# Eight of 31 convolution taps as diagonal products on TensorE, and a written-out order for VectorE beside the query, key and value products

## The chip, the cores and the metric

The program runs on one core of a Trainium2 chip. The metric is the device time of one execution in microseconds (us). A core has TensorE (PE, matrix products, 128x128 array that can be addressed in tiles of 32x32), VectorE (DVE), ScalarE (ACT), GpSimd (POOL) and SyncE (SP), which here issues the DMAs. Each engine runs its instructions in the order in which they stand in its queue, and semaphores order the engines against each other. SBUF is the working memory. PSUM, where TensorE writes its results, has eight banks of 128 partitions x 512 fp32 columns; POOL can't read it.

## The reference, cut to what matters

The model is a stack of blocks in fp32; the change touches the first mixer only. It takes 512 latent and 256 context rows of 1024 features (768 rows in all), projects them, and forms a convolution branch and query, key and value:

```python
def conformer_conv(p_glu, conv_w, conv_b, ln_g, ln_b):
    a, gate = jnp.split(p_glu, 2, axis=-1)
    u = depthwise_conv(a * jax.nn.sigmoid(gate), conv_w, conv_b)   # 31 taps, 512 channels
    return jax.nn.silu(layer_norm(u, ln_g, ln_b))
...
    conv_lat = conformer_conv(p_lat[..., :EV_Q0], conv_w, conv_b, ln_g, ln_b)
    q_lat = apply_axial_rope(qk_heads(p_lat[..., EV_Q0:EV_K0]), rope)
    k_lat = apply_axial_rope(qk_heads(p_lat[..., EV_K0:EV_V0]), rope)
    v_lat = v_heads(p_lat[..., EV_V0:])
```

The attention over all 768 keys follows, and the output projection takes the convolution and the attention side by side. Context rows go through the same convolution, without rotation of q and k.

## The kernel before, in words

Features lie on the 128 partitions, rows on the columns. An fp32 product is made of three fp32r products of high and low halves (`mm3`, lines 90 to 92). `wsplit` (line 60) loads a weight tile of 512 KB into `wraw` (3 buffers), ACT makes its high half `whi` (line 73), and DVE, or POOL where told, its low half `wlo` (line 74), two buffers of each. Before it loads, it advances a background generator by two steps: `mods` (line 146) makes modulation vectors, each from eight steps that load 512 KB of `ada_w` into `wraw` and run two fp32 products on 32-column strips of the array (line 153), and a ninth with a copy, four small products (line 160) and a DVE add (line 161).

`even_mixer` (line 355) first makes the gated input `us` of the convolution in four chunks of 128 channels (lines 414 to 424); beside it the generator `fg` makes the filters of a later block (`hyena_spectra`; its DVE lines here are 705, 719, 725 and 726, and its PSUM pool `evf` has 2 banks). Then comes the stage that the change touches. In it three streams are interleaved:

- `taps()` (line 437): per chunk, tap 0 has been made with the bias at line 424; taps 1 to 28 are 28 DVE instructions at line 449 over 128 x 798 columns (768 rows and the padding), each adding `us`, shifted by the tap, times a column of weights to `conv[i]`. Taps 29 and 30 are made by ACT (lines 443 and 446), POOL adds these two (line 447) and adds their sum to the chunk (line 452). After the fourth chunk `conv_norm` makes the layer norm over the channels and the SiLU, for 512 and then for 256 columns (lines 457 to 484). It is a generator that is advanced once or twice per product.
- eight q and k products: `wsplit`, 24 matmuls of 512 columns, rotation by three DVE instructions (494 to 496) and a POOL add (497), then 24 matmuls of 256 columns, copied by ACT (499). For the last four POOL makes the low half of the weight.
- twelve V products of 24 matmuls with 256 columns, two groups of six, each group with two weight tiles; ACT copies the results (511).

PSUM banks are handed out from below in the order in which pools are opened: `ps` has 4 banks, `mps` 2, `evf` 2 while the filters are made, and `cps`, for conv_norm, these 2 after it. Attention then opens pools over the same eight banks, with its score tiles `S` on banks 4 to 7. SBUF of pool `evp`, which the three streams use, lies where the filter generator's pool lay.

Nothing in the program fixes the order of the queues: a planner orders the instructions of all engines by program order and by its own model of durations, so that a later instruction may run ahead of an earlier one that waits.

Of the kernel before, what the change touches and what calls it, by code (L numbers as in the profile page):

```python
# [10 lines left out]
F32 = mybir.dt.float32  # L11
# [3 lines left out]
ALU = mybir.AluOpType  # L15
AX = mybir.AxisListType
PSUM = bass.MemoryType.PSUM

D = 1024
T = 512  # L20
C = 256
# [5 lines left out]
def f32(ap):  # L27
    return ap.bitcast(F32)

# [325 lines left out]
def even_mixer(k, xc):  # L355
    nc, a = k.nc, k.a
    regs = [(0, T), (T, C)]
# [8 lines left out]
    with ExitStack() as es:  # L366
        hp = es.enter_context(ExitStack())
        cp = es.enter_context(k.pool("evc"))
        tp_ = hp.enter_context(k.pool("evt", side="right"))
        ps = hp.enter_context(k.pool("evps", 4, space=PSUM))  # L370
        mps = hp.enter_context(k.pool("evmps", 2, space=PSUM))
# [4 lines left out]
        with k.pool("hyf") as hy, k.pool("evf", 2, space=PSUM) as fps:  # L376
# [5 lines left out]
            with k.pool("evn") as np_:  # L382
                rbs = [k.norm_stats([t], [rg], ps, np_)[0] for t, rg in zip((xl, xc), regs)]
                with k.pool("ada", side="right") as mp:
                    for i, _ in enumerate(chain(k.mods(0, 1, mps, mp, 12), k.mods(0, 0, mps, mp, 12))):
                        if i == 3:
                            next(fg)
                h1 = hp.enter_context(k.pool("evh", side="right"))
                hh = h1.tile([128, 8, TC], F32R, name="hh")
# [42 lines left out]
        def b3(dt=F32):  # L432
            return k.tmp([128, TC], "b3", dt, 8, vp)

        qk = [b3() for i in range(8)]
        with k.pool("evp") as pp, k.behind([k.mods(0, kind, mps) for kind in (2, 3, 4)], 2):
            def taps():

                for i in range(4):
# [8 lines left out]
                    for j in range(1, 29):  # L448
                        nc.vector.scalar_tensor_tensor(out=o, in0=u[:, j:j + W], scalar=cw[:, i, j:j + 1], in1=o, op0=ALU.mult, op1=ALU.add)
                        if j == 14:  # L450
                            yield
                    nc.gpsimd.tensor_tensor(out=o, in0=o, in1=o2, op=ALU.add)
# [33 lines left out]
            cps = hp.enter_context(k.pool("evcps", 2, space=PSUM))  # L486
            tg = taps()
            rope = k.cload("rope2d", [128, 2, T], pool=pp)
            for i in range(8):
                w = k.wsplit(a["ev_w_fm"][8 + i], eng=nc.gpsimd if i >= 4 else None)  # L490
                acc = k.gemm(w, h, 8, 0, T, ps)
                t1 = k.tmp([128, T], "rt1", bufs=1, pool=pp)
                t2 = k.tmp([128, T], "rt2", bufs=2, pool=pp)
                nc.vector.stream_shuffle(t2, acc, [(j + 16) % 32 for j in range(32)])
                nc.vector.tensor_tensor(out=t1, in0=acc, in1=rope[:, 0], op=ALU.mult)
                nc.vector.tensor_tensor(out=t2, in0=t2, in1=rope[:, 1], op=ALU.mult)
                nc.gpsimd.tensor_tensor(out=qk[i][:, 0:T], in0=t1, in1=t2, op=ALU.add)
                acc = k.gemm(w, h, 8, T, C, ps)
                nc.scalar.copy(qk[i][:, T:], acc)
                next(tg)  # L500
            for g in range(2):
                vb = [k.wsplit(a["ev_w_v"][g, kq * 4:kq * 4 + 4].rearrange("k p f -> p k f")) for kq in range(2)]
                for t in range(6):
                    acc = k.tmp([128, 512], "acc", pool=ps, bufs=None)[:, :256]
                    for kt in range(8):
                        s = slice(kt % 4 * 256, kt % 4 * 256 + 256)
                        w = vb[kt // 4]
                        k.mm3(acc, (hh[:, kt, t * 128:(t + 1) * 128], hl[:, kt, t * 128:(t + 1) * 128]),
                              (w[0][:, s], w[1][:, s]), kt == 0, kt == 7)
                    s = slice(g * 256, g * 256 + 256)  # L510
                    nc.scalar.copy(vv[:, t, s], acc)
                    if t % 3 == 2:
                        next(tg, None)
# [1737 lines left out]
```

## Time and profile before

| | us |
|---|---|
| median of 3 runs | 3662.72 (3659.55 to 3664.95) |
| the profiled execution | 3663.87, span 3662.1 |
| PE busy | 3421.9 (93% of the span) |
| DVE busy | 2431.2 (66%) |
| ACT busy | 1460.6 (40%) |
| POOL busy | 665.8 (18%) |

All times in the rows are counted from the start of the span. An engine's busy time is the union of its instructions, so that matmuls which overlap are counted once; `PEld` are TensorE's weight loads. `PEclk` is the granted clock of TensorE as a share of its full 2.4 GHz. An fp32 matmul leaves two records, an fp32r matmul one. The stage that the change touches lies between about 160 and 360 us.

### The profile page before, as it was taken

What the parts mean: (1) busy time and instruction counts of PE and PEld (TensorE: products, weight loads), DVE (VectorE), ACT (ScalarE), POOL (GpSimd) and SP (SyncE); (2) the same over time, 40 slices, a digit from 0 to 9 for tenths busy, and PEclk for the clock granted to TensorE, in tenths of its full rate; (3) what the DMA queues carried; (4) which work ended last, traced back from release to release, by engine and by line L of the source; (5) the groups of instructions that cost most, each with busy time, mean ns of one, the idle gap of its engine ahead of it and who ended that gap; (6) DMA issues with size and microseconds to landing.
All of it is one profiled execution on the core that took longest, in us unless ns stands there. A gap on an engine that the chain in (4) does not pass through costs nothing.

```text
span 3662.1 us, 54926 instructions
## 1 busy us (share of the span) xinstructions
PE 3421.9 (93%) x21924; PEld 2820.3 (77%) x21924; DVE 2431.2 (66%) x3995; ACT 1460.6 (40%) x2525; POOL 665.8 (18%) x587
## 2 busy tenths in 40 slices
PE   6987989999998899889999999999999999999999
PEld 3765878888887667667888877767998877777998
DVE  7997876544458765654334676657877676757886
ACT  4223543222226434323223444543444544644443
POOL 0042101102102332311111032021111032012110
PEclk9997999999999999889999999999999999999999
DMA  6334114333333222332223313232333313232333
GB/s 212 110 120 114 38 52 129 113 123 119 118 102 122 79 76 78 119 103 80 93 92 98 107 58 104 92 121 81 103 105 104 109 50 119 73 132 83 103 98 98
DMA packets 156842, 369.31 MB, mean 101 GB/s; under 512 B 19207, under 2 KB 44167, under 8 KB 156200
## 3 DMA queue, kind: packets, MB, share of 16 engines
q1 hardware_dynamic: 156584, 365.79, 31.5%
q8 instruction: 172, 2.82, 0.3%
q14 instruction: 86, 0.70, 0.1%
HBM read 334.27 MB, written 28.31 MB: 99 GB/s over the span
## 4 chain that ended last, share of the span: by engine, by line
PE 42%; DVE 12%; issue 6%; ACT 4%; POOL 2%; DMA 1%; SPq 0%; DVEq 0%; POOLq 0%; ACTq 0%
PE acc L90 12%; PE acc L92 12%; PE acc L91 12%; DVE wlo L74 1%; DMA wraw<-in_w_up_dram 1%; DVE hb L1614 1%; PE rec L1339 1%; PE rec L1340 1%; ACT whi L73 1%; DVE wslo L85 1%; PE acc L1416 1%; PE acc L1415 1%; DVE oz L830 1%; PE acc L1417 1%; ACT mp L1849 0%
## 5 line engine op out<-in xcount | busy, mean ns | idle before, releaser
L73 ACT CAST whi<-wraw 128x1024 fp32r<-128x1024 f32 (+2 forms) x442 | 408.0, 923 | 862.0 <-PE acc L91 664.4
L74 DVE TENSOR_TENSOR wlo<-wraw,whi 128x1024 fp32r<-128x1024 f32 (+2 forms) x438 | 487.1, 1112 | 185.4 <-ACT whi L73 180.7
L90 PE MATMUL acc<-hh,whi 128*128 128x512 f32 (+1 forms) x1024 | 367.4, 359 | 11.8 <-ACT whi L73 6.4
L92 PE MATMUL acc<-hh,wlo 128*128 128x512 f32 (+1 forms) x1024 | 364.9, 357 | 12.2 <-POOL wlo L74 8.8
L91 PE MATMUL acc<-hl,whi 128*128 128x512 f32 (+1 forms) x1024 | 365.8, 358 | 2.7 <-DVE hl L256 2.3
L91 PE MATMUL acc<-hidl,whi 128*128 128x512 f32 (+1 forms) x768 | 274.2, 357 | 1.6 <-DVE hidl L85 1.6
L92 PE MATMUL acc<-hidh,wlo 128*128 128x512 f32 (+1 forms) x768 | 274.2, 357 | 0.6 <-DVE wlo L74 0.6
L90 PE MATMUL acc<-hidh,whi 128*128 128x512 f32 (+1 forms) x768 | 274.4, 357 | 0.0
L341 POOL TENSOR_TENSOR sqr<-relu 128x512 f32<-128x512 f32 (+1 forms) x96 | 127.8, 1332 | 689.3 <-ACT relu L339 685.8
L90 PEld LDWEIGHTS acc<-hh,whi 128*128 128x128 f32 x1024 | 196.2, 192 | 50.9 <-ACT whi L73 10.2
L92 PEld LDWEIGHTS acc<-hh,wlo 128*128 128x128 f32 x1024 | 195.5, 191 | 47.0 <-POOL wlo L74 10.1
L91 PEld LDWEIGHTS acc<-hl,whi 128*128 128x128 f32 x1024 | 196.9, 192 | 35.4 <-DVE hl L256 5.9
L92 PE MATMUL acc<-shh,wlo 128*128 128x512 f32 (+1 forms) x480 | 194.7, 406 | 7.2 <-DVE wlo L74 7.2
L90 PE MATMUL acc<-shh,whi 128*128 128x512 f32 (+1 forms) x480 | 196.1, 409 | 3.5 <-ACT whi L73 3.5
L91 PE MATMUL acc<-shl,whi 128*128 128x512 f32 (+1 forms) x480 | 194.8, 406 | 1.1 <-issue 1.1
L85 POOL TENSOR_TENSOR flo<-fth,fhi 128x512 fp32r<-128x512 f32 x44 | 82.3, 1870 | 531.4 <-ACT fhi L84 506.5
L90 PE MATMUL acc<-fsh,wshi 128*128 128x256 f32 x576 | 163.7, 284 | 4.4 <-ACT wshi L84 4.4
L91 PEld LDWEIGHTS acc<-hidl,whi 128*128 128x128 f32 x768 | 145.1, 189 | 25.2 <-DVE hidl L85 2.0
L92 PE MATMUL acc<-fsh,wslo 128*128 128x256 f32 x576 | 162.5, 285 | 1.5 <-DVE wslo L85 1.5
L91 PE MATMUL acc<-fsl,wshi 128*128 128x256 f32 x576 | 163.4, 284 | 0.0
L92 PEld LDWEIGHTS acc<-hidh,wlo 128*128 128x128 f32 x768 | 144.3, 188 | 23.9 <-DVE wlo L74 1.0
L191 DVE SCALAR_TENSOR_TENSOR mdacc<-wraw,cs,mdacc 128x1024 f32<-128x1024 f32 x70 | 94.4, 1372 | 102.6 <-DMA wraw<-in_ada_w_dram 102.6
(684 smaller groups left out, 9142.8 us busy)
## 6 DMA issues: line engine op xcount, KB each, us to landing
wraw<-in_mlp_w_dram SPq DMA_DIRECT2D x128, 512.0 KB, 3.5
wraw<-in_ada_w_dram SPq DMA_DIRECT2D x96, 512.0 KB, 4.0
wraw<-in_w_in_dram SPq DMA_DIRECT2D x58, 512.0 KB, 3.5
wraw<-in_od_w_fm_dram SPq DMA_DIRECT2D x36, 512.0 KB, 3.6
wraw<-in_w_gate_dram SPq DMA_DIRECT2D x72, 256.0 KB, 2.9
wraw<-in_w_up_dram SPq DMA_DIRECT2D x72, 256.0 KB, 3.1
wraw<-in_w_down_dram SPq DMA_DIRECT2D x48, 256.0 KB, 2.7
wraw<-in_w_down_dram SPq DMA_DIRECT2D x32, 320.0 KB, 2.9
```

Of the source, the lines that this page charges most:

```text
L73: nc.scalar.copy(hi, raw)
L74: (eng or nc.vector).tensor_tensor(out=lo, in0=raw, in1=f32(hi), op=ALU.subtract)
L85: (eng or nc.vector).tensor_tensor(out=lo, in0=src, in1=f32(hi), op=ALU.subtract)
L90: nc.tensor.matmul(out, s[0], m[0], start=first, stop=False)
L91: nc.tensor.matmul(out, s[0], m[1], start=False, stop=False)
L92: nc.tensor.matmul(out, s[1], m[0], start=False, stop=last)
L191: nc.vector.scalar_tensor_tensor(out=acc, in0=w, scalar=c, in1=acc, op0=ALU.mult, op1=ALU.add)
L341: nc.gpsimd.tensor_tensor(out=s, in0=r, in1=r, op=ALU.mult)
L830: nc.vector.scalar_tensor_tensor(out=o, in0=p[:, j:j + n], scalar=w[:, j:j + 1], in1=o, op0=ALU.mult, op1=ALU.add)
L1339: nc.tensor.matmul(op_[pf[d], hd], qd[:, c, pf[d]], S[:, c], start=True, stop=False)
L1340: nc.tensor.matmul(op_[pf[d], hd], at[pf[d], c], vn[pf[d], hd], start=False, stop=True)
L1415: nc.tensor.matmul(o, hh[:, kt, ts], w[0][:, ws], start=first, stop=False)
```

## The change

Of each chunk's 31 taps, 21 to 28 become products: `dia` holds for each of 32x32 blocks the diagonal of the tap's weights, and `strips` runs, per chunk and region, 4 blocks of channels x 4 tap groups on the 16 tiles of the array, twice, into four banks; ACT copies them out, and `joined` adds the four tap groups with the matrix `sum4` and adds the result to `conv[i]` on DVE. DVE keeps taps 1 to 20. The chunk's sum with taps 29 and 30 goes from POOL to DVE, as do the low halves of the last four q and k weights.

`ps` has three banks now, the modulations' pool `mps` is closed after the first two vectors and opened anew with one bank, and `cps`, with four, is opened ahead of the taps. The taps advance one instruction per step, and inside `manual_schedule` DVE executes the instructions in the order in which the program states them; other DVE instructions may fall between them, and the other engines are left to the planner. The next weight is loaded and split ahead of the taps of a product.

```diff
+P0, PT = 21, 8
...
-        ps = hp.enter_context(k.pool("evps", 4, space=PSUM))
-        mps = hp.enter_context(k.pool("evmps", 2, space=PSUM))
+        ps = hp.enter_context(k.pool("evps", 3, space=PSUM))
...
-                with k.pool("ada", side="right") as mp:
+                with k.pool("ada", side="right") as mp, k.pool("evmps", 2, space=PSUM) as mps:
...
+        mps = hp.enter_context(k.pool("evmps1", 1, space=PSUM))
+        cps = hp.enter_context(k.pool("evcps", 4, space=PSUM))
         with k.pool("evp") as pp, k.behind([k.mods(0, kind, mps) for kind in (2, 3, 4)], 2):
+            dia = pp.tile([128, 4, PT, 32], F32, name="cdia")
+            for i in range(4):
+                nc.gpsimd.tensor_tensor(out=dia[:, i], in0=k.sum4.unsqueeze(1).to_broadcast([128, PT, 32]),
+                                        in1=cw[:, i, P0:P0 + PT].unsqueeze(2).to_broadcast([128, PT, 32]), op=ALU.mult)
+            def strips(i, r):
+                c0, n = regs[r]
+                bank = [k.tmp([128, 512], "acc", pool=cps, bufs=None) for _ in range(4)]
+                for t in range(0, PT, 4):
+                    for s in range(4):
+                        for q in range(4):
+                            p = slice(32 * q, 32 * q + 32)
+                            u0 = c0 + 30 * r + P0 + t + s
+                            nc.tensor.matmul(bank[q][32 * s:32 * s + 32, :n], dia[p, i, t + s], us[p, i, u0:u0 + n], start=t == 0, stop=t + 4 >= PT)
+                e = k.tmp([128, 4, T], "cve", bufs=1, pool=pp)
+                for q in range(4):
+                    nc.scalar.copy(e[:, q, :n], bank[q][:, :n])
+                return i, r, e
+            def joined(i, r, e):
+                c0, n = regs[r]
+                acc = k.tmp([128, 512], "acc", pool=ps, bufs=None)[:, :n]
+                for q in range(4):
+                    nc.tensor.matmul(acc[32 * q:32 * q + 32], k.sum4, e[:, q, :n], start=True, stop=True)
+                o = conv[i][:, c0 + 30 * r:c0 + 30 * r + n]
+                nc.vector.tensor_tensor(out=o, in0=acc, in1=o, op=ALU.add)
...
-                    for j in range(1, 29):
+                    last = strips(i, 0)
+                    for j in range(1, P0):
                         nc.vector.scalar_tensor_tensor(out=o, in0=u[:, j:j + W], scalar=cw[:, i, j:j + 1], in1=o, op0=ALU.mult, op1=ALU.add)
-                        if j == 14:
-                            yield
-                    nc.gpsimd.tensor_tensor(out=o, in0=o, in1=o2, op=ALU.add)
+                        if j == P0 // 2:
+                            joined(*last)
+                            last = strips(i, 1)
+                        yield
+                    nc.vector.tensor_tensor(out=o, in0=o, in1=o2, op=ALU.add)
+                    joined(*last)
                     yield
...
-            for i in range(8):
-                w = k.wsplit(a["ev_w_fm"][8 + i], eng=nc.gpsimd if i >= 4 else None)
-                acc = k.gemm(w, h, 8, 0, T, ps)
...
-                next(tg)
...
+            with k.tc.manual_schedule(engines={mybir.EngineType.DVE}):
+                some(12)
+                w = k.wsplit(a["ev_w_fm"][8])
+                for i in range(8):
+                    accs = [k.gemm(w, h, 8, c0, n, ps) for c0, n in regs]
+                    if i < 7:
+                        w = k.wsplit(a["ev_w_fm"][9 + i])
+                    else:
+                        vb = [k.wsplit(a["ev_w_v"][0, kq * 4:kq * 4 + 4].rearrange("k p f -> p k f")) for kq in range(2)]
+                    some(5)
+                    acc = accs[0]
...
+                for g in range(2):
+                    for t in range(6):
...
+                        some(3 if g else 2)
+                    if g == 0:
+                        vb = [k.wsplit(a["ev_w_v"][1, kq * 4:kq * 4 + 4].rearrange("k p f -> p k f")) for kq in range(2)]
             for _ in tg:
                 pass
```

`some(n)` advances `taps()` by n steps. The rotation, the copies and the twelve V products are as before.

## Rows read from the trace of the kernel before

**Rows 1.** The page's first line.
```profile
span 3662.1 us, 54926 instructions
```
**Rows 2.** Stretches from 80 to 372 us, busy time of each engine.
```profile
core 0: us, PE busy (x) PEld busy (x) DVE busy (x) ACT busy (x) POOL busy (x), PEclk, DMA share, GB/s
80.00:160.00 80.00, 72.82 (x367) 58.22 (x366) 75.97 (x100) 23.80 (x37) 2.59 (x2) 0.96 0.27 86
160.00:191.00 31.00, 28.18 (x127) 18.05 (x126) 31.00 (x39) 5.45 (x7) 3.40 (x2) 1.00 0.52 170
191.00:296.00 105.00, 80.06 (x404) 57.44 (x404) 102.43 (x101) 19.20 (x26) 44.69 (x19) 0.85 0.36 116
296.00:352.00 56.00, 49.46 (x356) 44.30 (x356) 40.06 (x58) 22.46 (x41) 18.51 (x13) 0.88 0.50 140
```
**Rows 3.** The same for line 449 alone, the taps.
```profile
80.00:160.00 80.00, 29.90 (x29) 0.96 0.27 86
160.00:191.00 31.00, 9.81 (x9) 1.00 0.52 170
191.00:312.00 121.00, 96.30 (x74) 0.84 0.35 113
```
**Rows 4.** Timeline of TensorE: start, duration, engine, line, operation, idle before.
```profile
211.18 1.06 PE L153 MATMUL acc<-wraw,cs 128*32 128x512 f32 x8
...
212.17 0.50 PE L90 MATMUL acc<-hh,whi 128*128 128x512 f32 x1
...
217.87 0.28 PE L90 MATMUL acc<-hh,whi 128*128 128x256 f32 x1
...
220.70 0.95 PE L160 MATMUL acc<-c_ada_sel,wraw 128*128 128x4 f32 x8
...
251.09 0.79 PE L92 MATMUL acc<-hh,wlo 128*128 128x512 f32 x1 [8.28 <-POOL wlo L74]
...
354.74 0.77 PE L571 MATMUL S<-KS,QS 128*128 128x512 f32 x1 [1.10 <-issue]
```
**Rows 5.** Groups of POOL's instructions, 120 to 300 us: busy, mean ns | idle before.
```profile
L497 POOL TENSOR_TENSOR b<-rt,rt 128x512 f32<-128x512 f32 x8 | 15.8, 1980 | 28.5 <-DVE rt L496 28.5
...
L447 POOL TENSOR_TENSOR cw<-cw,cw 128x798 f32<-128x798 f32 x4 | 10.1, 2523 | 24.8 <-ACT cw L446 24.8
L452 POOL TENSOR_TENSOR conv<-conv,cw 128x798 f32<-128x798 f32 x3 | 7.7, 2565 | 19.3 <-DVE conv L449 19.2
```
**Rows 6.** Timeline of DVE.
```profile
117.46 8.73 DVE L449 SCALAR_TENSOR_TENSOR conv<-xl,c_ev_conv_w,conv 128x798 f32<-128x798 f32 x9
...
188.36 1.28 DVE L719 SCALAR_TENSOR_TENSOR hys<-acc,hyinv 128x512 f32<-128x512 f32 x2
...
295.23 1.21 DVE L74 TENSOR_TENSOR wlo<-wraw,whi 128x1024 fp32r<-128x1024 f32 x1
...
342.90 0.16 DVE L467 TENSOR_SCALAR ms<-acc 128x2 f32<-128x2 f32 x1 [0.67 <-PE acc L465]
...
352.98 1.66 DVE L479 SCALAR_TENSOR_TENSOR conv<-acc,c_ev_ln,conv 128x256 f32<-128x256 f32 x4
...
357.56 0.75 DVE L483 SCALAR_TENSOR_TENSOR conv<-cv,conv 128x256 f32<-128x256 f32 x2
```
**Rows 7.** Groups of DVE's instructions, 191 to 312 us.
```profile
L494 DVE STREAM_SHUFFLE rt<-acc 128x512 f32<-128x512 f32 x8 | 5.8, 737 | 0.0
L495 DVE TENSOR_TENSOR rt<-acc,c_rope2d 128x512 f32<-128x512 f32 x8 | 5.4, 678 | 0.5 <-POOL b L497 0.5
```
**Rows 8.** Timeline of TensorE in a later block.
```profile
1218.15 0.75 PE L1239 MATMUL prep<-R,LM 32*32 32x32 f32 x64
```
**Rows 9.** Groups of instructions by shape, 165 to 360 us.
```profile
L479 DVE SCALAR_TENSOR_TENSOR conv<-acc,c_ev_ln,conv 128x512 f32<-128x512 f32 x4 | 2.7, 744 | 1.1 <-PE acc L121 1.1
...
L157 ACT COPY wraw<-acc 128x512 f32<-128x512 f32 x3 | 1.8, 585 | 9.5 <-PE acc L153 9.5
...
L479 DVE SCALAR_TENSOR_TENSOR conv<-acc,c_ev_ln,conv 128x256 f32<-128x256 f32 x4 | 1.7, 477 | 0.0
```

More of the change, by code (lines that the diff above doesn't have):

```diff
@@ L484, in conv_norm @@
                 yield
-            cps = hp.enter_context(k.pool("evcps", 2, space=PSUM))
             tg = taps()
             rope = k.cload("rope2d", [128, 2, T], pool=pp)
-            for i in range(8):
-                w = k.wsplit(a["ev_w_fm"][8 + i], eng=nc.gpsimd if i >= 4 else None)
-                acc = k.gemm(w, h, 8, 0, T, ps)
[L492 to L499, printed above, removed]
-                next(tg)
@@ L501, in even_mixer, with some @@
[L501 to L513, printed above, removed]
+            def some(n):
+                for _ in range(n):
+                    next(tg, None)
@@ new lines, in even_mixer @@
+            with k.tc.manual_schedule(engines={mybir.EngineType.DVE}):
[9 more added lines that the diff above has]
+                    acc = accs[0]
+                    t1 = k.tmp([128, T], "rt1", bufs=1, pool=pp)
+                    t2 = k.tmp([128, T], "rt2", bufs=2, pool=pp)
+                    nc.vector.stream_shuffle(t2, acc, [(j + 16) % 32 for j in range(32)])
+                    nc.vector.tensor_tensor(out=t1, in0=acc, in1=rope[:, 0], op=ALU.mult)
+                    nc.vector.tensor_tensor(out=t2, in0=t2, in1=rope[:, 1], op=ALU.mult)
+                    nc.gpsimd.tensor_tensor(out=qk[i][:, 0:T], in0=t1, in1=t2, op=ALU.add)
+                    nc.scalar.copy(qk[i][:, T:], accs[1])
+                for g in range(2):
+                    for t in range(6):
+                        acc = k.tmp([128, 512], "acc", pool=ps, bufs=None)[:, :256]
+                        for kt in range(8):
+                            s = slice(kt % 4 * 256, kt % 4 * 256 + 256)
+                            w = vb[kt // 4]
+                            k.mm3(acc, (hh[:, kt, t * 128:(t + 1) * 128], hl[:, kt, t * 128:(t + 1) * 128]),
+                                  (w[0][:, s], w[1][:, s]), kt == 0, kt == 7)
+                        s = slice(g * 256, g * 256 + 256)
+                        nc.scalar.copy(vv[:, t, s], acc)
+                        some(3 if g else 2)
+                    if g == 0:
+                        vb = [k.wsplit(a["ev_w_v"][1, kq * 4:kq * 4 + 4].rearrange("k p f -> p k f")) for kq in range(2)]
```

## The prediction, made before the changed kernel ran

> **What bounds the kernel now.** I read the span first, then the busy time of each engine by stretch, then the vector engine (DVE) inside the stage that the change touches, then TensorE's long waits there. The profiled execution lasted 3663.87 us with a span of 3662.1 us [rows 1], 1.77 us around it; the median of the runs is 3662.72, so this execution lies 1.15 above it, and I take that off at the end. Over the kernel TensorE is busy nearly everywhere; this stage is one of the exceptions, and the reader is to see it in [rows 2]: from 191 to 296 us DVE works 102.43 of 105 us and TensorE only 80.06. DVE is the bound there, with the taps: 74 of the 112 tap instructions run in 191 to 312 and take 96.30 us [rows 3]. The other 38 had already run, 29 of them in 80 to 160 and 9 in 160 to 191, between instructions of the gate products and of the filter generator. TensorE's longest single wait, 8.28 us, is for a weight's low half that GpSimd (POOL) makes [rows 4]; POOL had stood 19.2 us behind taps, at the chunk sum of L452 [rows 5]. Once the taps are over, the V products and the convolution's norm run side by side (296 to 352), and attention begins when the norm lets go of its banks: the last reading of a broadcast bank by L479 ends at 352.98 + 1.66 = 354.64, and the second score tile starts at 354.74 [rows 4, 6]. So what counts is the time at which conv_norm ends.
>
> **Step 1, taps.** 32 of 112 tap instructions go. Nine in a row take 8.73 us [rows 6], so .97 each and 31 us in all. Added on DVE: four chunk sums that POOL did (estimate .9 each, just under a tap, which has the same width) and eight joining adds (.68 for 512 columns, as L495 takes [rows 7], and about .42 for 256, an estimate: 4.4 us), 8.0 us; and four weight halves at 1.21 that POOL made, 4.8 us. POOL loses these eight instructions, the products of `dia` come to it (four, early, beside nothing).
>
> **Step 2, strips.** A strip of 512 columns is 32 matmuls in two rounds of 16 array positions. The nearest row is L153: four fp32 matmuls of 512 columns on four column groups, eight records, take 1.06 us together [rows 4]. That positions on different rows of the array overlap too is shown by L1239, whose 64 records of 32x32 lie on four positions, no two on the same rows, and take .75 us [rows 8]. If all 16 overlap, a strip costs 2.1 us (1.1 for 256 columns); if only the four columns do, 8.5 and 4.2. I take the lower, since each of the two directions overlaps in its row; the two at once no row shows. `joined` is the pattern of L153 itself: 1.06 and .6. Together 4.9 us a chunk, 19.5 us on TensorE; the bad end is 57 us.
> The Trainium skill (TensorE: Matmul & The Clock Gate, Part 3: Packing small matmuls) states a 10.6-fold gain for 16 positions at 512 columns; by it a strip would be 32 x 1.06 / 10.6 = 3.2 us, an estimate, and the stage some 4 us longer. The sum does not use it.
>
> **Step 3, the given order.** Instructions keep their order on DVE. The first twelve taps stand before the low half of the first weight (w8), and behind tap 10 stands the joining add of strip (0,0). This strip needs four PSUM banks. With `ps` on banks 0 to 2 the filters' pool is 3 and 4, `evmps1` is 3 and `evcps` 4 to 7, so one strip bank, and the evicted copy's place in SBUF too, come free only with the filter generator. Its last two evictions end at 188.36 + 1.28 = 189.64 [rows 6]. So ten taps run early instead of 38 by 191, and behind the waiting add stand two taps, w8, and with it all eight products; TensorE and SP's weight loads wait for that.
> The generator ends earlier in exchange: DVE was busy all 31.00 us of 160 to 191 [rows 2], 9.81 of them in taps [rows 3], which now stand still. I give it 6 of these (between 0 and 9.8, since its matmuls, casts and POOL adds also follow one another): 183.6. Then strip 2.1, four copies by ACT at .585 [rows 9] 2.3, joined 1.06, add .68, semaphores about .5: 190.3. Two taps 2.0, w8 1.2: 193.5. There 68 taps are left, where 74 were left in the kernel before at 191, and no product has begun. Of the 32 taps saved, six remain as a gain at this point. In 80 to 160, 19 fewer taps can free at most the 7.2 us for which TensorE is idle there [rows 2], and a bank less in `ps` can take some back: I count 0 and keep -5 to +3 for the range.
>
> **Step 4, the eight products.** TensorE needs for one 217.87 - 212.17 = 5.70 and 220.70 - 217.87 = 2.83 [rows 4], two modulation steps .53 each, and 5 of a chunk's 21 steps of strips, 1.2: 10.8. DVE needs w 1.2, five taps 4.85, rotation .74 + 2 x .68 = 2.1 [rows 7], adds .5: 8.6, and more while POOL works beside it: the 74 taps took 96.30 us instead of 72, 24 us more under 44.69 us of POOL [rows 2, 3], about half a us each; POOL keeps 15.8 + 10.1 us [rows 5], so about 1.4 per product. 10.0 against 10.8: TensorE sets the pace and DVE, which can't pull later taps ahead, idles. Twice the add of the modulations (L161) stands ahead of a weight half and waits for a matmul behind a whole product: 3 us. 193.5 + 8 x 10.8 + 3 = 283.
>
> **Step 5, V.** The second V half needs the buffer of the last weight, free at 283, and five taps, rotation 7 and twelve steps stand behind it: cast and half 2.3, taps 17 x .97 = 16.5, rotation 2.1, adds 1.8, POOL 1: 306.7. Only then come the halves of the second V group, 2.4, then the last 20 taps, 19.4, adds 2.0, waits 1.5: 332. V ends on TensorE ahead of that, near 327, where in the kernel before it went on up to 352 [rows 2].
>
> **Step 6, the tail.** conv_norm now lies alone behind the taps, in order, and its four last steps each wait for two ACT instructions. The 256-column half took, from L467 at 342.90 to the end of L483 at 358.31, 15.4 us [rows 6], some 4 of it other work; its three sums add 1.2. The 512 half scales by L479's forms, 744 / 477 = 1.56 [rows 9]. I take 16 + 26 = 42 us (between 35 and 47): end at 374, the last bank 3.7 us earlier (358.31 - 354.64) at 370. Against 354.64 this is 16 us later. Little hides it: all four score banks are banks of `evcps`, and the output products need conv. After it the rest of the kernel is unchanged and bound by TensorE, so the shift stays. 3662.72 + 16 = 3679.
>
> **Rivals.** (a) DVE doesn't idle: TensorE and the weight loads keep ahead of it. For it speaks that POOL's waits, 8.28 us in one place, are gone. Then DVE's own work decides: from 193.5, 68 taps 66, eleven halves 13.3, rotations 16.7, adds 7.3, POOL 10, so 307, plus 42, less 3.7: 345, 9 us earlier than 354.64; with a generator 4 us earlier and a tail of 37 us 18 earlier. 3645 to 3654, middle 3650: faster. It decides from the point where the products' period falls below 10.0 us or the fixed halves arrive without the waits of step 5. Against it stands that each rotation waits for a product by its place in the order.
> (b) The tail is covered: conv_norm's four rotating banks free the first score tile some 10 us before the last one, so that TensorE takes scores while the norm ends, and half of DVE's idling goes: no change, 3662. Against it: the first output product needs conv.
> (c) The strips don't overlap on the rows: 57 - 19.5 = 38 us more on TensorE, about 25 on the path: 3704.
> That an edit does nothing at all I can exclude for the taps; the order on the other engines stays the planner's and can move it by some us either way.
>
> **Numbers.** The forecast 3679 (3669 to 3695) has .50, (a) .25, (b) .15, (c) .10. What a measurement can tell from no change is 0.2%, 7.3 us. Slower .60, same .15, faster .25. The range, 3640 to 3706, takes in (a) with its best tail and (c).
>
> **What would show it.** Right: the first joining add starts within 10 us after the filters' last eviction; at that point only ten taps have run; the first product starts after 190; a gap on TensorE of over 30 us, filled with norm matmuls alone, between the last V product and the first score; conv_norm over 35 us long. Strips near 2 us each show step 2. Wrong: a first product before 180, taps that end before 315, or scores that begin before 350; then (a) holds. A strip over 6 us is (c).

## The result, and the profile after

The changed kernel takes 3716.99 us (median of 4 runs, 3708.53 to 3722.84) against 3663.27 us of the kernel before on the same chip: ratio 1.0146, 95% interval 1.0123 to 1.0169, some 54 us slower. The forecast was 3679 in a range up to 3706: the direction is right, the size is three times too small. The profiled execution took 3713.8 us, 49.9 more than that of before. All of it arises ahead of attention: the first score matmul starts at 402.05 us instead of 352.69, 49.4 later, and from there to the end of the span both kernels need the same time (3712.0 - 402.05 = 3309.95, 3662.1 - 352.69 = 3309.41). Of the 49.4 us, 23.3 have gathered when the eighth product ends (294.0 against 270.7), and 26.1 between there and the first score.

The stretches of the changed kernel, busy time of each engine (as [rows 2]):
```profile
core 0: us, PE busy (x) PEld busy (x) DVE busy (x) ACT busy (x) POOL busy (x), PEclk, DMA share, GB/s
80.00:160.00 80.00, 73.09 (x356) 58.74 (x355) 56.57 (x79) 22.33 (x34) 2.58 (x2) 0.94 0.26 86
160.00:191.00 31.00, 22.16 (x107) 16.08 (x106) 23.94 (x30) 5.89 (x8) 6.75 (x6) 0.89 0.25 85
191.00:296.00 105.00, 97.33 (x806) 67.47 (x806) 67.47 (x80) 27.16 (x46) 16.97 (x11) 0.97 0.37 121
296.00:352.00 56.00, 53.61 (x525) 38.76 (x525) 41.26 (x44) 12.57 (x27) 2.03 (x1) 1.00 0.33 104
352.00:372.00 20.00, 7.75 (x49) 5.77 (x47) 17.59 (x22) 8.44 (x12) 6.06 (x4) 0.61 0.58 178
372.00:402.00 30.00, 7.99 (x32) 7.20 (x32) 19.56 (x36) 10.59 (x19) 9.69 (x9) 0.50 0.21 48
```
DVE and TensorE have changed places. From 191 to 296 DVE, which was full, is busy 67.47 of 105 us and TensorE 97.33. From 352 to 402, where TensorE had scores to do, it is busy 15.74 of 50 us at a granted clock of .61 and .50 (half is 1.2 of 2.4 GHz, the lower level): what is left is a join and the last modulation matmuls, until 356.2, and then the norm's small matmuls alone. The taps alone, line 487 (as [rows 3]):
```profile
80.00:160.00 80.00, 10.43 (x10) 0.94 0.26 86
160.00:191.00 31.00, 0.00 (x0) 0.89 0.25 85
```
Ten taps ran early where 38 had. DVE's timeline (as [rows 6]) then shows the path: the filters' last eviction, a wait for the first joining add (L471), the two taps and the low halves behind it, four waits behind the last product (5.12, 7.41, 4.94 and 1.12 us), the last add, and the norm's last reading of a bank:
```profile
188.73 1.37 DVE L770 SCALAR_TENSOR_TENSOR hys<-acc,hyinv 128x512 f32<-128x512 f32 x2
...
208.05 0.69 DVE L471 TENSOR_TENSOR conv<-acc,conv 128x512 f32<-128x512 f32 x1 [16.59 <-PE acc L469]
208.78 2.14 DVE L487 SCALAR_TENSOR_TENSOR conv<-xl,c_ev_conv_w,conv 128x798 f32<-128x798 f32 x2
210.83 2.35 DVE L78 TENSOR_TENSOR wlo<-wraw,whi 128x1024 fp32r<-128x1024 f32 x2
...
297.12 0.17 DVE L165 TENSOR_TENSOR mods<-acc,c_ada_b 128x16 f32<-128x16 f32 x1 [5.12 <-PE acc L164]
...
305.84 1.22 DVE L78 TENSOR_TENSOR wlo<-wraw,whi 128x1024 fp32r<-128x1024 f32 x1 [7.41 <-ACT whi L77]
...
335.82 1.23 DVE L78 TENSOR_TENSOR wlo<-wraw,whi 128x1024 fp32r<-128x1024 f32 x1 [4.94 <-ACT whi L77]
...
356.21 0.17 DVE L165 TENSOR_TENSOR mods<-acc,c_ada_b 128x16 f32<-128x16 f32 x1 [1.12 <-PE acc L164]
...
361.56 0.42 DVE L471 TENSOR_TENSOR conv<-acc,conv 128x256 f32<-128x256 f32 x1
...
400.29 1.66 DVE L520 SCALAR_TENSOR_TENSOR conv<-acc,c_ev_ln,conv 128x256 f32<-128x256 f32 x4 [1.27 <-PE acc L125]
```
TensorE's timeline tells what the first join waited for (as [rows 4]): modulation weights that stand ahead of the strip, the strip at a low clock, ACT's copies. The join itself is then cut up by pieces of the next strip and takes from 203.44 to 208.01, 4.57 us, where one in a single piece takes 1.07 (at 342.59). The first score follows .10 us behind that last bank reading (400.29 + 1.66 = 401.95):
```profile
189.47 1.06 PE L157 MATMUL acc<-wraw,cs 128*32 128x512 f32 x8
195.34 1.92 PE L157 MATMUL acc<-wraw,cs 128*32 128x512 f32 x4 [4.81 <-DMA wraw<-in_ada_w_dram]
197.20 3.28 PE L458 MATMUL acc<-xl,cdia 32*32 32x512 f32 x64
200.41 1.05 PE L157 MATMUL acc<-wraw,cs 128*32 128x512 f32 x4
203.44 1.53 PE L469 MATMUL acc<-cve,sum 128*32 128x512 f32 x4 [1.98 <-ACT cve L461]
204.90 0.61 PE L458 MATMUL acc<-xl,cdia 32*32 32x256 f32 x2
205.45 1.05 PE L469 MATMUL acc<-cve,sum 128*32 128x512 f32 x2
206.43 0.61 PE L458 MATMUL acc<-xl,cdia 32*32 32x256 f32 x2
206.97 1.04 PE L469 MATMUL acc<-cve,sum 128*32 128x512 f32 x2
...
229.32 2.35 PE L458 MATMUL acc<-xl,cdia 32*32 32x512 f32 x64
...
342.59 1.07 PE L469 MATMUL acc<-cve,sum 128*32 128x512 f32 x8
...
402.05 0.77 PE L622 MATMUL S<-KS,QS 128*128 128x512 f32 x1 [1.88 <-issue]
```
In the waits of 7.41 and 4.94 us ACT has no V weight to cast yet. The queue of SyncE, which issues the loads, shows why: two loads of modulation weights (`ada_w`) stand ahead of each of these V weights.
```profile
295.29 2.19 SPq L154 DMA_DIRECT2D wraw<-in_ada_w_dram  x2
298.46 0.38 SPq L74 DMA_DIRECT2D wraw<-in_ev_w_v_dram  x1
...
327.91 0.80 SPq L154 DMA_DIRECT2D wraw<-in_ada_w_dram  x2
330.31 0.38 SPq L74 DMA_DIRECT2D wraw<-in_ev_w_v_dram  x1
```
In the kernel before, the low half of the first product's weight is made at 172.28, beside the filter generator, and two of the eight products are through by 198.5. From the timelines of that kernel, two rows that the prediction did not use, of DVE and of TensorE (the first matmul of the third product):
```profile
172.28 1.98 DVE L74 TENSOR_TENSOR wlo<-wraw,whi 128x1024 fp32r<-128x1024 f32 x1
...
198.65 0.40 PE L90 MATMUL acc<-hh,whi 128*128 128x512 f32 x1
```

### The profile page after: what moved, and what is told of

It reads as the page before. It is cut to its first block, busy times and chain, and to the rows that moved or that the text cites. A ratio compares the mean times of both kernels' runs of the same rounds, so it can differ in the third digit from the quotient of the medians.

```text
span 3712.0 us, 56106 instructions
## 1 busy us (share of the span) xinstructions
PE 3444.2 (93%) x22500; PEld 2827.6 (76%) x22500; DVE 2405.6 (65%) x3979; ACT 1475.9 (40%) x2557; POOL 640.0 (17%) x583
## 4 chain that ended last, share of the span: by engine, by line
PE 39%; DVE 14%; issue 7%; ACT 4%; POOL 2%; DMA 2%; SPq 0%; DVEq 0%; ACTq 0%; POOLq 0%
PE acc L94 11%; PE acc L96 11%; PE acc L95 10%; DVE wlo L78 2%; DMA wraw<-in_w_up_dram 1%; DVE wslo L89 1%; ACT whi L77 1%; DVE hb L1665 1%; PE rec L1390 1%; PE rec L1391 1%; DVE wlo L89 1%; PE rec L1375 1%; DVE oz L881 1%; DVE ws L1973 0%; DVE xl L2076 0%
## 5 line engine op out<-in xcount | busy, mean ns | idle before, releaser
L95 PEld LDWEIGHTS acc<-hidl,whi 128*128 128x128 f32 x768 | 144.7, 188 | 26.1 <-DVE hidl L89 2.6
L94 PEld LDWEIGHTS acc<-hidh,whi 128*128 128x128 f32 x768 | 144.1, 188 | 23.5
```

Source lines behind the costliest of these rows:

```text
L94: nc.tensor.matmul(out, s[0], m[0], start=first, stop=False)
L95: nc.tensor.matmul(out, s[0], m[1], start=False, stop=False)
```

## The experiments

Each kernel has 4 runs (E11, E14 and E17 have 10) and is measured against 4 to 13 runs of the kernel before on the same chip; the theories are those written ahead of each run. The marks below are read from the timeline of one profiled execution each, in us: start of the eighth product's last matmul (.28 us long), end of the last addition to conv, start of the first and of the last score matmul. The last two columns are the median and the ratio with its interval. The four runs of a kernel lie up to 23 us apart, so that differences of a few us between two changed kernels show nothing.
```
                                products  conv   first   last     us     ratio
before                            270.7   313.4  352.7  477.0   3663.3
changed                           294.0   362.0  402.0  526.1   3717.0  1.0146 [1.0123, 1.0169]
E1  w8 before join                280.8   349.1  389.2  513.1   3712.2  1.0131 [1.0108, 1.0153]
E2  seven items per product       294.7   345.6  400.0  523.1   3723.8  1.0167 [1.0146, 1.0188]
E3  E1 and E2                     285.9   338.3  394.5  517.9   3716.0  1.0144 [1.0125, 1.0163]
E4  no given order                300.9   360.7  400.1  524.0   3726.0  1.0171 [1.0143, 1.0200]
E5  order without strips          277.6   360.2  395.6  520.4   3698.5  1.0101 [1.0086, 1.0116]
E6  product before join           278.7   346.8  387.0  510.9   3703.3  1.0111 [1.0096, 1.0127]
E7  taps early, joins late        306.4   334.8  391.1  527.5   3724.9  1.0171 [1.0156, 1.0186]
E8  changed, no modulations       288.1   339.4  375.5  499.3   3696.2  1.0101 [1.0084, 1.0118]
E9  norm in other banks           290.1   358.6  369.6  514.2   3710.8  1.0139 [1.0121, 1.0157]
E10 E6 and E9                     278.0   345.5  355.4  501.2   3697.5  1.0101 [1.0084, 1.0119]
E11 before, no modulations        262.9   309.9  346.2  470.1   3658.3  0.9994 [0.9984, 1.0003]
E12 changed, no norm              292.4   362.4  374.8  498.7   3685.5  1.0062 [1.0038, 1.0087]
E13 strips in the old order       309.5   314.5  373.9  498.3   3691.1  1.0075 [1.0058, 1.0092]
E14 before, no norm               269.5   311.3  338.2  459.4   3657.1  0.9981 [0.9972, 0.9990]
E15 E10, fewer steps per weight   269.1   328.8  369.3  495.7   3693.7  1.0086 [1.0071, 1.0101]
E16 E15, six items per product    270.8   323.7  351.9  500.0   3698.6  1.0104 [1.0087, 1.0122]
E17 before, three banks           279.5   318.4  360.2  487.4   3668.9  1.0021 [1.0010, 1.0031]
E18 E13, four banks, join later   299.7   304.7  362.8  488.8   3678.7  1.0044 [1.0028, 1.0060]
```

**E1, the first weight ahead of the first join.**
```diff
-                some(12)
+                some(9)
```


> Changed kernel with nine taps instead of twelve items ahead of the query/key/value products, so that the low half of the first weight stands in VectorE's order before the first joining add. Theory A (three terms: a late first product, a TensorE that is full from there to the last V product, the normalization alone behind it): first product at 190 to 197 us instead of 212, everything behind it 15 to 18 us earlier, three items more left for the end (about +3 us): 3700 to 3706 us. Rival B (TensorE's work, strips and joins included, must be done before the scores whatever the order, and it is what is late): under 5 us, 3712 or more. Rival C (the first product waits for the cold strip and the modulation weights on TensorE, not for the add): the first product stays past 205.

The low half comes early now and the first product runs at 172 to 189, beside the generator, earlier than any theory said. But the second waits until 206.39: TensorE has it behind the join, and the join behind ACT.
```profile
200.64 2.89 PE L469 MATMUL acc<-cve,sum 128*32 128x512 f32 x6 [4.14 <-ACT cve L461]
...
206.39 0.50 PE L94 MATMUL acc<-hh,whi 128*128 128x512 f32 x1
```
The first score comes 12.8 us earlier, as A said, but the median falls by only 5, which by itself is B's range, and the profiled span by 0.6: the lead is still 9.5 us at 2040 and 3.2 at 3000. Behind the start of attention both kernels have the same instructions in the same order on TensorE and DVE, so this is taken for the spread between executions (E1's runs lie from 3703.7 to 3718.3). The marks in the stage are therefore read beside each time below. For the stage B is out; C, whose first product was to stay past 205, holds for the second.

**E6, the product ahead of the join on TensorE too.**
```diff
-                some(12)
+                some(9)
-                        if j == P0 // 2:
+                        if j == (P0 // 2 if i else 17):
```


> Nine taps ahead as in the first experiment, and the first joining add of group 0 behind its tap 17 instead of tap 10, so that TensorE too has the first product ahead of the first join (which needs ScalarE's copies of the strip). Theory F: the first product was late because TensorE sat idle between strip and join; it starts at 195 to 200 instead of 206, first score 380 to 384 (389 in the first experiment), 3695 to 3705 us. Rival G (the pace is set by weights and modulations, not by that gap): first product earlier but first score at 387 or later.

The product after the strip, the second, starts at 196.14; the first score is at 387.0, on the line between F and G, the median falls by 13.7 us and lies in F's range. The join's place costs about 14 us (15 at the first score).
```profile
193.50 2.35 PE L458 MATMUL acc<-xl,cdia 32*32 32x512 f32 x64
196.14 0.50 PE L94 MATMUL acc<-hh,whi 128*128 128x512 f32 x1 [0.29 <-ACT whi L77]
```

**E2 and E3, more items beside each product.**
```diff
-                    some(5)
+                    some(7)
```


> Changed kernel with seven items of the convolution beside each of the eight products instead of five, so that the 84 items end within the V products and the normalization stands in VectorE's order beside the second half of V. Theory A: TensorE, not VectorE, sets the pace of the products (81.9 busy of 82 us), so they stay within 82 to 86 us; the normalization overlaps the last six V products and of its 45 us some 10 to 20 stay behind the last V product: 25 to 35 us less than the changed kernel, 3682 to 3692 us. Rival D (VectorE is the bound of the products): each product grows by its two taps, 16 us in all, and about 10 us of gain is left: 3700 to 3710.

> Both edits: nine taps ahead, seven items beside each product. Theory A: the two terms add, 15 to 18 us at the start and 22 to 32 at the end: 3667 to 3680 us, near the kernel before. If TensorE's work is the only bound (rival B), nothing beyond what seven items alone give: 3682 to 3692.

Theory A fell in both, and so did the rivals D and B, whose ranges lie below both medians. The convolution ends 16 and 24 us earlier, but from there to the first score it takes 54 and 56 us instead of 40: the norm's small matmuls now stand in TensorE's queue between the V products and hold them until DVE or POOL has delivered (5.9 us of waits between 349 and 368 in E2). The last V product ends at 366 in E2 instead of 353. The norm's overlap with V was not worth what A counted.

**E4, E5 and E13, one part alone.** E4 takes the written order away and keeps strips, counts and emission; E5 keeps the order and takes the strips away; E13 is the kernel before with strips, its own order, the new PSUM pools and the chunk's sum on DVE. E5 also has one item more beside each V product, not shown below.
```diff
-            with k.tc.manual_schedule(engines={mybir.EngineType.DVE}):
+            with ExitStack():
```
```diff
-P0, PT = 21, 8
+P0, PT = 29, 0
...
-                    some(5)
+                    some(7)
```
```diff
+                    last = strips(i, 0)
-                    for j in range(1, 29):
+                    for j in range(1, P0):
-                        if j == 14:
+                        if j == P0 // 2:
+                            joined(*last)
+                            last = strips(i, 1)
```


> Changed kernel without the order given for VectorE: the same instructions, ordered on all engines by the planner as in the kernel before. Theory A (the order is what holds the low half of the first weight behind the joining add, pauses the taps beside the filter generator and puts the normalization last): the taps run beside the generator again (over 70 of 80 us busy in 80 to 160), TensorE's strips remain, and the time falls to 3660 to 3690 us. Rival E (the strips and joins on TensorE and the three PSUM banks are the cost, not the order): within 10 us of 3717.

> The given order of VectorE alone: the changed kernel with all 28 taps of a channel group on VectorE again and no strip or join on TensorE (PSUM as in the changed kernel; seven items beside each product, three and four in V, since there are 116 items now instead of 84). Theory F (the taps end too late because those that stood beside the filter generator now stand behind it, and the normalization's chain of 40 us follows the last tap): first product at 190 to 197; 104 items of 1.05 us, the rope work (17 us) and the weights' low halves (14 us) behind it end the taps at 335 to 350, first score 375 to 390: 3688 to 3703 us, slower than before without any strip. Rival E (the strips and joins are the cost, since the planner's order with strips was as slow as the written one): within 10 us of the kernel before, 3655 to 3674.

> The strips alone: the kernel before with its own program order (two steps per channel group, one beside each product, no written order), eight taps per group as strips on TensorE with the first join behind tap 10 and the second behind tap 20, and the changed kernel's PSUM pools. Theory F (the strips are cheap and the order is the loss): VectorE loses 24 us net of joins in a stage where it was 78.5 of 79 us busy and TensorE 58.9, so the taps end 10 to 25 us earlier than 313; first score 335 to 362, 3645 to 3672 us. Rival E (strips, copies and joins lock TensorE's queue whatever the order): first score 380 or later, 3690 or more.

E4 is against A: 35 taps ran by 193 and the convolution still ends at 361, for DVE then waits for weights (their high halves, 32.8 us in all), for products (18.8 us) and for joins (L471, 16 us). At 3726 it is in E's range: with strips, counts and emission as they are, leaving the order to the planner gains nothing. E5 has F's time, 36 us slower without a single strip; its last addition at 360 and first score at 396 are later than F said. E13 is in E's range, 28 us slower, with a first score (373.9) between both theories: its convolution ends at 314.5, 1 us later than in the kernel before, and it is TensorE that is late (products until 309.5). So each part loses by itself, the order 36 and the strips 28 us, and together 54. Both contain the three banks of the gate products, which alone cost some 7 us (E17 below).

**E7, as many early taps as before and the joins spread.** `taps()` emits 38 items ahead of the first product and one join per five items from item 44 on.
```diff
-                some(12)
+                some(38)
+                        if n >= J0 and (n - J0) % 5 == 0:
+                            if last:
+                                joined(*last)
+                            last = strips(*q.pop(0)) if q else None
```


> 38 taps ahead of the first product, as many as the kernel before ran by then, and the eight joining adds spread from item 44 on, one per five items, instead of tied to taps 10 and 20 of their group; everything else as in the changed kernel. Theory F: over 70 of 80 us of VectorE busy in 80 to 160, first product at 190 to 200, last tap at 300 to 325, first score 345 to 370 (402 in the changed kernel, 353 before): 3655 to 3680 us. Rival E (TensorE's strips are the cost): taps end early but V and with it the first score stay above 385: 3700 or more.

A miss. Only 20 taps ran early: item 21 is the sum of ACT's and POOL's taps, and in the given order everything behind it, the first weight too, waits for it.
```profile
193.32 0.99 DVE L488 TENSOR_TENSOR conv<-conv,cw 128x798 f32<-128x798 f32 x1 [3.91 <-POOL cw L483]
```
The experiment did not test what it was meant to; it shows the same fault at another place.

**E8 and E11, the modulations left out of the changed kernel and of the kernel before.**
```diff
-        with k.pool("evp") as pp, k.behind([k.mods(0, kind, mps) for kind in (2, 3, 4)], 2):
+        with k.pool("evp") as pp, k.behind([], 2):
+            for kind in (2, 3, 4):
+                k.md[0, kind] = k.mpool.tile([128, 8, 2], F32, name=f"mods0_{kind}")
+                nc.gpsimd.memset(k.md[0, kind], 0.0)
```


> Changed kernel with the three modulations (kinds 2, 3 and 4 of the first layer) left out: their 24 weight loads, 192 matmuls and three adds are not run and zeros stand in their place. Theory F: what remains of the delay is the order: the first product still waits for strip, copies and join (200 to 208), V's weights come without a wait, taps end 15 to 25 us earlier than 361, first score 375 to 387: 3690 to 3705 us. Rival G (the loads ahead of the weights and strips on SyncE's queue are the cause): first product before 197 and first score before 365: under 3682.

> The kernel before with the same three modulations left out (zeros in their place) as in the eighth experiment, which gave 21 us against the changed kernel. Theory J (they cost the changed kernel more because its TensorE is full there and its V weights wait behind their loads): the kernel before gains under 12 us, 3650 or more. Rival K (they cost both kernels the same): 18 to 25 us, 3637 to 3645.

F and J hold. From the last product to the last addition the changed kernel needs 51 us without them and 68 with them. They cost it 20.8 us and the kernel before 4.1, which is within its interval of nothing. Of DVE's four waits behind the last product none is left in E8; the one wait for a weight there, 9.10 us, ends about 1 us after that product. So those waits come from the modulations' loads, matmuls and adds.

**E12 and E14, the normalization left out of both.**
```diff
-                for r in range(2):
-                    yield from conv_norm(r)
```


> Changed kernel with the normalization, gate and rescaling of the convolution's output left out (the raw sums go on). Theory F: everything up to the last tap stays (taps end 355 to 362, V 347 to 353) and the first score follows within 10 us of it, at 360 to 372 instead of 402: 3678 to 3690 us. If the stage is bound elsewhere (weights, the stacked queries and keys), first score above 385.

> The kernel before without the normalization, gate and rescaling of the convolution's output, as the twelfth experiment for the changed kernel (which gained 32 us). Theory F: in the kernel before it runs beside V, whose last product ends at 350, so it gains 0 to 12 us: 3650 to 3662. Rival K (it costs both kernels the same): 25 us or more, under 3638.

F holds in both, but for the first score (374.8, 3 us late in E12). The norm is worth 31.5 us against 6.5 in the medians; at the first score 27.3 against 14.5. The norm alone behind the taps is worth between 13 and 25 us more than beside V. With nothing but the stacked queries and keys behind the last addition, the score still starts 12.4 us after it.

**E9 and E10, the norm in banks that the scores do not take.**
```diff
-                mu = k.tmp([128, 512], "acc", pool=cps, bufs=None)
+                mu = k.tmp([128, 512], "acc", pool=ps, bufs=None)
```
(and the same for both broadcasts and `rinv`; E10 has the edits of E6 as well)

> Changed kernel whose normalization takes its PSUM from the three banks of the products (ps) instead of the four of the strips (cps); nothing else. In the trace of the changed kernel the first score starts 0.10 us after the normalization's last read of a cps bank (402.05). Theory H (the 40 us of the normalization sit on the path only because the score tiles take over its banks): the first score starts 25 to 45 us earlier, at 357 to 377, the normalization runs beside the attention, and the time falls by 15 to 35 us to 3682 to 3702. Rival I (the scores wait for the normalization itself or for the stacked queries and keys in any bank): first score above 395, within 8 us of 3717.

> The sixth experiment (first product ahead of the first join, 196 us) and the normalization in the other banks together. Theory H: the terms add: first score 340 to 362, about where the kernel before has it (353), and the attention carries the normalization's VectorE and ScalarE work: 3655 to 3685 us. Rival I: as the sixth alone, 3695 to 3708.

The bank is what holds the first score: it moves from 402 to 369.6, as H said. But the time falls by 6 us only, with runs that overlap those of the changed kernel, and the last score comes 11.9 earlier, not 32: the second score matmul runs at 379.27, and the norm's steps now take their turns among the scores'. H is right on the bank and wrong on its worth; the norm's work has to be done before or within attention. E10 repeats this: its first score, 355.4, is where H said, and its time, 3697.5, is I's, 6 us below E6.
```profile
369.62 0.77 PE L622 MATMUL S<-KS,QS 128*128 128x512 f32 x1 [2.21 <-DMA KS<-KS]
...
379.27 0.77 PE L623 MATMUL S<-KS,QS 128*128 128x512 f32 x1
```

**E15 and E16, fewer modulation steps per weight, and six items per product, on E10.**
```diff
-        with k.pool("evp") as pp, k.behind([k.mods(0, kind, mps) for kind in (2, 3, 4)], 2):
+        with k.pool("evp") as pp, k.behind([k.mods(0, kind, mps) for kind in (2, 3, 4)], 1):
```
```diff
-                    some(5)
+                    some(6)
```


> The tenth experiment (product first, normalization in the other banks: 3698 us) with one step of the modulations per weight instead of two, so that 15 of the 27 steps follow behind the normalization, beside the attention. Theory F (their loads and matmuls delay strips and V's weights): V ends 10 us earlier, first score 342 to 350, 3683 to 3693 us. Rival L (what is taken out here stands in the attention's way): 3697 or more.

> As the fifteenth, with six items beside each product instead of five, so that the last tap comes with the last V product and not 9 us behind it. Theory F: 4 to 8 us below the fifteenth, 3677 to 3688. Rival M (VectorE is full beside the products, or the normalization then stands in TensorE's queue ahead of V as with seven items): no better than the fifteenth, 3686 or more.

V ends at 323 and 326, 27 to 30 us earlier than in the changed kernel, and in E16 the first score is where the kernel before has it (in E15 it is not, 369). The time does not follow: 3693.7, between F's range and L's, and 3698.6, which is M. What was taken out of the stage now runs beside attention, as L has it, and the last score comes 19 and 23 us later than in the kernel before. That this work is what delays the scores is argued from its place; the marks show that terms found by single removals do not add when the work is only put elsewhere.

**E17 and E18, the banks of the gate products.**
E17 is the kernel before with
```diff
-        ps = hp.enter_context(k.pool("evps", 4, space=PSUM))
+        ps = hp.enter_context(k.pool("evps", 3, space=PSUM))
```
and E18 is E13 with
```diff
+        ps = us_ps.enter_context(k.pool("evps0", 4, space=PSUM))
...
+        us_ps.close()
...
-                        if j == P0 // 2:
+                        if j == (P0 // 2 if i else 17):
```


> The kernel before with three PSUM banks instead of four for its products (ps), nothing else. Theory N (the bank is what delays the gate products by 6 us): TensorE 12 to 15 us busy in 60 to 80 instead of 18.0, the filter generator's last eviction 4 to 7 us later, 3664 to 3672 us. Rival O (the planner's shuffle, not the bank): 16 or more of 20 us busy there and 3658 to 3666.

> The thirteenth experiment (strips in the old order, 3691 us) with four banks for the gate products, closed before the strips open theirs, and the first join behind tap 17 of the first group, so that the second product stands ahead of it. Theory F: the generator ends at 190 to 192 again, the products follow without the gap (second product before 205 instead of 215), first score 352 to 362: 3665 to 3680 us. Rival E (TensorE's added 20 us are the loss): no more than 6 us gained, 3685 or more.

N and F hold (E18's first score is 0.8 us past F's range, and E17's median is in N's alone). With one bank less the gate products end 5.4 us later; their last gate, of E17 and then of the kernel before:
```profile
165.50 0.42 DVE L422 SCALAR_TENSOR_TENSOR xl<-th,acc 128x256 f32<-128x256 f32 x1
```
```profile
160.09 0.42 DVE L422 SCALAR_TENSOR_TENSOR xl<-th,acc 128x256 f32<-128x256 f32 x1
```
E18 gains 12.3 us on E13 with the banks and the later join, and is the best kernel with strips: 17 us slower than before. It is TensorE that is full in it, where DVE was [rows 2]:
```profile
191.00:296.00 105.00, 98.51 (x925) 60.75 (x925) 77.34 (x85) 29.14 (x54) 29.26 (x15) 0.97 0.31 96
```
No kernel that does all the work beat the kernel before.

## Why the prediction was wrong

The chain of steps was the right one, and the marks for "right" came but for one: ten taps early, no product before 190, 49 us between the last V product and the first score (the first 3 of them with a join and modulation matmuls), the norm 40 us long behind the taps. The one that failed is the first joining add within 10 us of the last eviction: it began 18 us behind it. Two terms were mis-sized, the way to the first join in step 3 and the "waits 1.5" of step 5. The absolute times of the steps against the trace, and what each adds:

- Step 2 held: a strip 2.35 us (1.50 for 256 columns) where 2.1 and 1.1 stood, nearer to the 2.1 of the sum than to the 3.2 beside it, and a join 1.07, each in one piece; rival (c) is out. Cut into pieces they cost more, as the first join did.
- Step 3 failed by 18.5 us. The first weight's low half ends at 212.0 instead of 193.5. 6.5 us are the generator, whose last eviction ends at 190.10 and not at 183.6. The pausing taps gave some 4 of the 6 us counted for them: in E1 and E3, whose last gates come where those of before do, the last eviction ends 3.7 and 4.3 us earlier. But here the gate products ended at 166 instead of 160. I had put the lost bank into the range (-5 to +3) and counted it at 0; E17 shows +5.4 for it. It is not the bank alone: E1, E3 and E6 have three banks too and end their last gates at 161 to 162, so what the planner makes of three banks decides, and why it differs stays open. 12 us are the join: I had strip, copies, join and add follow each other from the last eviction on without a gap (6.7 us), and 18.6 passed. 7.1 went by until the strip began at 197.20, with 4.81 us of idle time and the matmuls of modulation weights ahead of it; the cold strip took 3.28 instead of 2.1; from its end to the join's first matmul it was 3.0 instead of 2.3, with a weight's cast and a tap ahead of ACT's copies; and the join, cut up by pieces of the next strip, took 4.57 instead of 1.06. The .5 us of that sum for semaphores rests on no row. E6 gives back 13.7 us.
- Step 3 also compared wrongly: "no product has begun" is true of the changed kernel, but the kernel before had done two by 198.5, which is worth more than the six taps that I counted as left over. The sum did not use it; a look at the first low half in the trace would have warned me.
- Step 4 was 7.5 us too dear, and by luck hid part of the rest: 82.0 us from 212.0 to 294.0 instead of 89.5. TensorE sets the pace, as said: it is busy 81.89 of the 82 us.
- Step 5 failed by 19 us: 68 us from the last product to the last addition instead of 49. "Waits 1.5" stood for 5.12 + 7.41 + 4.94 + 1.12 = 18.6 us. E8 takes the modulations out and measures 51. I had charged their add 3 us among the products and none in V, and had not followed their loads, which stand ahead of V's weights in SyncE's queue.
- Step 6 held: 40 us from the last addition to the last bank instead of 38.

18.5 - 7.5 + 19 + 2 = 32, the difference between a last bank at 370 and at 402. The rest of the distance from 16 to 54 is 1.95 us (the first score of before starts ahead of its last bank), and the 4 us by which the medians differ more than the profiled executions.

Rival (a) failed at its stated condition: DVE idles, 19 of 82 us beside the products and 18 of 68 behind them. Rival (b) was half right: E9 shows that scores can begin 32 us earlier, and that it is worth 6 or less.

By removal the join's place (13.7), the modulations (20.8 - 4.1) and the norm (31.5 - 6.5) come to 55 us, about the whole; but E15 and E16, which mend parts of all three, still lose 30 to 35, so they overlap. What the 17 us of E18 are is argued from its full TensorE, not shown; an estimate from the rows has eight strips and joins at 4 x (2.35 + 1.50 + 1.07 + .64) = 22 us of TensorE's time if each runs in one piece, of the size of the loss. A version with all 38 early taps and no wait among them was not run.

## What to carry to other kernels

In an order that is written out, each instruction that waits for another engine is a gate for everything behind it: follow what the waiting one needs (here a strip, behind modulation weights, copied by ACT) on every queue before giving it a place, and put the first weight of the next stage, and its first products, ahead of it in both queues (E1 did the first alone and moved the first score by 13 us, E6 both and moved it by 15). In this kernel, work taken off the full engine was no gain, and the engine that received it was full afterwards (97.33 of 105 us where 80.06 had been); count both engines after the change, not the one before. A forecast of "waits 1.5" over 50 us of an in-order queue should be made wait by wait.

## What the runs showed of the hardware that was not expected

64 records of 32x32 positions take 2.35 us in one piece at a granted clock of 1.00 (229 to 232 us). They took 3.28 when TensorE had been idle for 4.81 us shortly before, at a granted clock of .68 from 197 to 201 us, part of it at the lower level, 1.2 GHz. Cut up, they cost more, and so does what they are put between (the first join, 4.57 us instead of 1.07): the strip of 304 to 327 us ran in five pieces among V products, and a piece of two records held TensorE as long as one of 26, 308.72 to 309.69 against 306.18 to 307.23 at the next product:
```profile
306.18 1.12 PE L458 MATMUL acc<-xl,cdia 32*32 32x512 f32 x26
307.23 0.38 PE L95 MATMUL acc<-wlo,hh 128*128 128x256 f32 x1
...
308.72 1.04 PE L458 MATMUL acc<-xl,cdia 32*32 32x512 f32 x2
309.69 0.39 PE L94 MATMUL acc<-whi,hh 128*128 128x256 f32 x1
```
The pieces of 8, 26, 2, 2 and 26 together took 5.4 us where one piece takes 2.35.
